# Adding the experts' rows to the residual by an accumulating scatter, with the final norm as a pass of its own

## The chip, the cores and the metric

The kernel runs on one core of a Trainium2 chip. The time is the device time of one execution in microseconds, the median of the runs shown. The engines are TensorE (PE, its weight loads PEld), VectorE (DVE), ScalarE (ACT), GpSimd (POOL) and SyncE (SP); SP, ACT and POOL issue DMAs, which run on the core's 16 DMA engines.

## What is computed

One layer of an encoder on 2048 tokens of 1024 numbers: a norm, a projection, two groups of attention heads, an output projection that is added to the input, and then a mixture of 64 SwiGLU experts. The change touches only what comes after the output projection:

```python
h = h + mixed @ w_out[l]
h = h + hier_moe(rms_norm(h, norm2_gain[l]), ...)      # 8 groups of 8 experts
return rms_norm(h, final_gain)

def hier_moe(x, ...):
    # each token: the best group, in it the best two experts, each with a gate
    expert_id = g_idx[:, None] * EXPERTS_PER_GROUP + top_idx
    ...
    h = silu(xb @ w_gate[e]) * (xb @ w_up[e]); ys = h @ w_down[e]
    y = zeros.at[slot_tok].add(ys * slot_gate[:, None])
```

A token's two experts are always of the same group. The last line makes the output out of the residual plus two gated expert rows.

## The kernel before

The attention stage goes over 16 tiles of 128 tokens and, for each, writes three things to memory: the residual rows (to the output tensor, `out2`, lines 1016 and 1153), the normed rows `d_xn`, and for each of a token's two experts a record in a list `d_list`, which has 100 slots for each expert. A record holds four numbers: the token, the gate, and two flags, "this is the token's last expert" and "its first". `route` (line 1195) works the record out; for the last two tiles the list is made by matmuls (`list_columns`, line 1298), two columns at a time, so that the list `L` is in SBUF when the experts begin.

The expert stage (`experts`, line 1476) goes over 64 experts in an order that visits the eight groups in turn, so that two experts of the same group are eight visits apart. An expert's three weight matrices are 2 MB each and come as six halves of 1 MB (`loads`, into nine `raw` buffers, issued from SP). ScalarE casts a half to `wh`, VectorE subtracts it from the original to give `wl` (`weights`), and TensorE multiplies three times for each product (`products`: `pg`, `pu`, `py`). `inputs` gathers up to 100 normed rows of the expert into `xg` by an indirect DMA from GpSimd and transposes them; `silu` makes `hh` and `hT`.

`sums` (line 1603) closes an expert: it gathers the tokens' rows so far from `out2` into `rg`; VectorE adds the gated product, `r = py * gate + rg`; ScalarE squares `r` and sums, and scales `gf`, the final gain, by the flags; GpSimd makes the norm's factor of the sum with three small instructions; VectorE multiplies, `o = r * ss * o`; and a scatter from GpSimd writes `o` to `out2`. With a first expert the flags make factor and gain one, so that `r` itself is written; with the last one the normed row is written, which is the output. A gather waits for the scatter of the same group's expert before (`data_dep`, eight visits back); the others are declared free of each other.

The order of the instructions on TensorE, VectorE, ScalarE and GpSimd is fixed ahead by `Plan` (line 121): every step is a generator that asks for an engine with a duration and what it needs (`ask`), and `Plan.run` picks the step that can start first. Each engine then works through its list in that order. After the experts, `nblk` says whether any expert had over 100 tokens; a loop for these follows under `tc.If`, and doesn't run with this data.

Of the kernel before, what the change touches and what calls it, by code (L numbers as in the profile page):

```python
# [8 lines left out]
F32 = mybir.dt.float32  # L9
# [19 lines left out]
NG = 8  # L29
# [167 lines left out]
def hybrid_encoder_kernel(ctx, tc, x, norm1_gain, w_in, gla_up_fwd, gla_up_fwd_bias, gla_up_bwd,  # L197
# [20 lines left out]
    L = pers.tile([CAP, NE, 4], I32, name="L")  # L218
# [5 lines left out]
    rec_a = pers.tile([P, NT, 2, 4], I32, name="rec_a")  # L224
# [24 lines left out]
    d_list = scratch("d_list", [LROWS + OROWS, 4], I32)  # L249
# [559 lines left out]
    with ExitStack() as ph:  # L809
# [163 lines left out]
        def project(i, t):  # L973
# [25 lines left out]
            for j in range(2):  # L999
# [16 lines left out]
                nc.sync.dma_start(out2[i * P:(i + 1) * P, j * 512:(j + 1) * 512], hs[j])  # L1016
# [123 lines left out]
        def last_rows(t):  # L1140
# [8 lines left out]
            for j in range(2):  # L1149
# [3 lines left out]
                nc.sync.dma_start(out2[i * P:(i + 1) * P, js], hs[j])  # L1153
# [41 lines left out]
        def route(i, lg, t):  # L1195
# [59 lines left out]
            tr = t  # L1255
            v.tensor_tensor(acc, acc, ob, op=OP.add)
            give(t, f"rank{i - 1}")
            if i in order[-2:]:
# [6 lines left out]
                tr = yield from list_columns(i, 0, o12, at, vals, t, tg)  # L1265
            t = yield ask("dve", 0.7, t, tg)
# [12 lines left out]
            t = yield ask("dve", 0.1, t)  # L1279
# [11 lines left out]
            if i == order[-3]:  # L1291
                t = yield ask("pool", 1.04, t)
                nc.gpsimd.dma_start(L, d_list[0:LROWS].rearrange("(p e) c -> p e c", p=CAP))
                t = yield ask("dve", 0.15, landed(t, 5.0))
                v.tensor_copy(L0, L[:, :, 0])
                give(t, f"list0of{i - 1}", f"list2of{i - 1}")

        def list_columns(i, c0, o12, at, vals, *t):
# [4 lines left out]
            for c in range(2):  # L1303
                src = tok[:, i:i + 1].to_broadcast([P, 2]) if c0 + c == 0 else rows[:, :, c0 + c].bitcast(F32)
                nc.vector.tensor_tensor(vals[:, :, c], o12, src.rearrange("p (k o) -> p k o", o=1).to_broadcast([P, 2, NE]),
                                        op=OP.mult)
            t = yield ask("pe", 0.25, t, take=("pt", f"list{c0}of{i}"))
# [4 lines left out]
            for c in range(2):  # L1312
                src = dst = L[:, :, c0 + c].bitcast(F32)
                if c0 + c == 0:
                    src, dst = L0, L[:, :, 0] if i == last else L0
                nc.vector.tensor_tensor(dst, pt[0:CAP, c], src, op=OP.add)
            give(t, "pt", f"list{c0}of{i - 1}")
# [103 lines left out]
    with ExitStack() as ph:  # L1421
# [5 lines left out]
        xgs, rgs = [], []  # L1427
        for lst, nm in ((xgs, "xg"), (rgs, "rg")):
            for j in range(2):
                t = wp.tile([CAP, D], F32, name=f"{nm}{j}")  # L1430
                nc.gpsimd.memset(t, 0.0)
                lst.append(t)
# [43 lines left out]
        def experts(blocks, ahead=(), then=None):  # L1476


            plan = Plan({"xg": 2, "rg": 2, "xT": 2, "hT": 2, "wh": WN, "wl": WN, "pt": 2, "pg": 1, "pu": 1, "py": PYN,
                         "hh": 2, "r": 2, "o": 2, "visit": NG, "raw": NAHEAD + NB - len(ahead)})  # L1480
            add, give = plan.add, plan.give
            raws, ws, xTs, hTs, ps, nb = {}, {}, {}, {}, {}, len(blocks)
            gets, puts = {}, {}
# [7 lines left out]

            def rows(e, t, out, src):
                return nc.gpsimd.indirect_dma_start(  # L1493
                    out=out, out_offset=None, in_=src, in_offset=bass.IndirectOffsetOnAxis(ap=column(e, 0), axis=0),
                    bounds_check=T - 1, oob_is_err=False)
# [26 lines left out]
            def inputs(e):  # L1522
                xg = xgs[e % 2]
                t = yield ask("pool", 1.95, listed_at, take=("xg",), urge=20.0)
                rows(e, t, xg, d_xn)
# [77 lines left out]
            def sums(e):  # L1603
                rg = rgs[e % 2]
                gate, last, first = (column(e, c) for c in (1, 2, 3))
                t = yield ask("pool", 1.75, listed_at, take=("visit", "rg"), urge=40.0)
                get = rows(e, t, rg, out2)
                for p in range(max(e - NG + 1, 0), e):
                    if p in puts:
                        tc.declare_no_dep(get.ins, puts[p].ins, reason="tokens of other groups")  # L1610
                if e >= NG:
                    tc.add_manual_dep(get.ins, puts[e - NG].ins.name, data_dep, reason="the group's expert before")
                gets[e] = get
                if e + 1 < nb:
                    add(sums(e + 1))
                tr = yield ask("dma", 1.18, (t[0] + 1.5, "pool"), urge=40.0)
                t = yield ask("dve", 1.28, (tr[0] + 1.8, "dma"), take=(f"py{e}", "r"), urge=40.0)
                r = sp.tile([CAP, D], F32, name="r")
                nc.vector.scalar_tensor_tensor(r, ps.pop((e, 2)).rearrange("p a b -> p (a b)"), gate, rg, op0=OP.mult,  # L1619
                                               op1=OP.add)  # L1620
                give(t, "py", "rg")
                o = sp.tile([CAP, D], F32, name="o")
                ss = sp.tile([CAP, 1], F32, name="ss")
                t = yield ask("act", 1.25, t, take=("o",), urge=40.0)
                nc.scalar.activation(o, r, AF.Square, accum_out=ss)
                tg = yield ask("act", 1.24, t, urge=40.0)
# [101 lines left out]
```

## Time and profile before

| | |
|---|---|
| three runs | 3051.7, 3054.0, 3058.02 us; median 3054.0 |
| profiled execution | 3056.35 us, its span 3054.6 us |
| mean granted clock of TensorE | 0.981 |
| busy in the span | PE 93%, DVE 77%, ACT 63%, POOL 27% |
| attention stage | to about 1665 us |
| expert stage | first `xg` transposed at 1702 us, last scatter issued at 3044 us |

In the slices of the page a digit is a busy share in tenths. A row of the timeline has start, duration, engine, line, operation, tiles and shapes; in brackets the idle time of the engine before it and what ended it. A line of the waits has who waited for whom: us in total, times, the longest. A line on a DMA queue has packets, MB and the share of the time of 16 engines that the packets took: q1 is SP's queue, which carries the weights, q0 is GpSimd's, which carries the gathered and scattered rows (it also has packets of 4 bytes, which is why its packets are more than its rows). Stretches for a gather or a scatter were chosen where nothing else was under way on q0.

### The profile page before, as it was taken

The numbers are of one execution on the slowest core, as the hardware profiler recorded it, in microseconds if no ns is written. First come the engines' busy times: TensorE is split into PE (matmuls) and PEld (weight loads), VectorE is DVE, ScalarE is ACT, GpSimd is POOL, SyncE is SP. The second block draws the span as 40 slices with busy tenths as digits, with TensorE's granted clock in tenths as the row PEclk, the third lists the DMA queues.
The fourth block names the chain that finished last, engine by engine and source line by source line (L and its number), as shares of the span: only waits on it lengthen the run. The fifth ranks groups of instructions, "written<-read, shape, count | busy, mean of one in ns | idle before, by whom it ended". The sixth has DMA issues, their size and how long they took to land. (4 is left out here: it accounts for less than half of the span.)

```text
span 3054.6 us, 39259 instructions
## 1 busy us (share of the span) xinstructions
PE 2844.3 (93%) x13784; PEld 2093.0 (69%) x13784; DVE 2365.0 (77%) x3430; ACT 1917.9 (63%) x2872; POOL 810.0 (27%) x575
## 2 busy tenths in 40 slices
PE   7999999999999999999998699899988988988987
PEld 6888788887677777777776466666666666666664
DVE  6554788888667767767776698888888888888886
ACT  4333333333777777777775587777777677777775
POOL 3443111111000000000001354434445444344433
PEclk9999999999999999999998799999999999999998
DMA  7874322223512222112124899999999999999994
GB/s 251 278 269 165 143 96 105 105 77 121 203 56 68 72 68 70 64 61 78 60 72 151 270 342 348 334 344 341 336 337 340 334 334 345 341 335 337 343 325 157
DMA packets 184135, 647.16 MB, mean 212 GB/s; under 512 B 45801, under 2 KB 60489, under 8 KB 130365
## 3 DMA queue, kind: packets, MB, share of 16 engines
q1 hardware_dynamic: 134462, 574.14, 54.3%
q0 software_dynamic: 35008, 51.28, 5.7%
q10 hardware_dynamic: 14464, 19.21, 1.9%
q8 instruction: 109, 1.79, 0.3%
q14 instruction: 92, 0.75, 0.1%
HBM read 563.96 MB, written 108.82 MB: 220 GB/s over the span
## 5 line engine op out<-in xcount | busy, mean ns | idle before, releaser
L1518 DVE TENSOR_TENSOR wl<-raw,wh 128x2048 fp32r<-128x2048 f32 x384 | 872.6, 2286 | 109.8 <-ACT wh L1516 108.1
L1516 ACT CAST wh<-raw 128x2048 fp32r<-128x2048 f32 x384 | 728.7, 1902 | 242.0 <-DMA raw<-in_w_up_dram 83.4
L1353 DVE TENSOR_TENSOR p_l<-p,p_h 128x512 fp32r<-128x512 f32 x512 | 343.7, 688 | 191.7 <-ACT p_h L1350 184.5
L1342 ACT ACTIVATE p<-ps 128x512 f32<-128x512 f32 x512 | 296.1, 599 | 149.1 <-PE ps L1339 130.3
L1563 PE MATMUL pg<-wh,xT 128*100 128x512 f32 x1024 | 357.0, 411 | 0.0
L682 DVE TENSOR_REDUCE nm<-pm 128x1 f32<-128x1024 f32 x256 | 304.8, 1215 | 43.6 <-PE pm L680 43.5
L1563 PE MATMUL pu<-wh,xT 128*100 128x512 f32 x1024 | 332.0, 395 | 0.0
L1569 PE MATMUL py<-wh,hT 128*100 128x512 f32 x1024 | 292.9, 398 | 5.9 <-DVE hT L1599 3.3
L1493 POOL DMA_INDIRECT rg<-out_dram,L x64 | 155.0, 2422 | 511.6 <-DVE r L1619 499.2
L1563 PE MATMUL pg<-wl,xT 128*100 128x512 f32 x512 | 212.0, 414 | 65.9 <-DVE wl L1518 65.6
L1350 ACT CAST p_h<-p 128x512 fp32r<-128x512 f32 x448 | 268.9, 624 | 5.8
L1285 POOL DMA_INDIRECT d_list<-rec_a,di x28 | 28.0, 1000 | 818.2 <-DVE di L1281 813.9
L1563 PE MATMUL pu<-wl,xT 128*100 128x512 f32 x512 | 206.3, 403 | 29.2 <-DVE wl L1518 29.0
L1569 PEld LDWEIGHTS py<-wh,hT 128*100 128x100 f32 x1024 | 167.1, 166 | 74.8 <-DVE hT L1599 7.9
L1563 PEld LDWEIGHTS pg<-wh,xT 128*100 128x100 f32 x1024 | 177.2, 173 | 58.0
L1563 PEld LDWEIGHTS pu<-wh,xT 128*100 128x100 f32 x1024 | 168.9, 165 | 64.0 <-ACT wh L1516 0.2
L1338 PE MATMUL ps<-q,K 128*128 128x512 f32 x512 | 210.6, 411 | 1.5 <-ACT p L1342 1.0
L1364 PE MATMUL pa<-p_h,V 128*66 128x512 f32 x512 | 204.3, 399 | 0.0
L1366 PE MATMUL pa<-p_l,V 128*66 128x512 f32 x512 | 202.7, 396 | 0.9 <-DVE p_l L1353 0.7
L1339 PE MATMUL ps<-q,K 65*128 65x512 f32 x512 | 203.2, 397 | 0.0
L1365 PE MATMUL pa<-p_h,V 128*64 128x512 f32 x512 | 201.6, 394 | 0.0
L1493 POOL DMA_INDIRECT xg<-d_xn,L x64 | 151.6, 2369 | 104.0 <-PE pt L1536 94.9
(426 smaller groups left out, 5730.6 us busy)
## 6 DMA issues: line engine op xcount, KB each, us to landing
raw<-in_w_gate_dram SPq DMA_DIRECT2D x128, 1024.0 KB
raw<-in_w_up_dram SPq DMA_DIRECT2D x128, 1024.0 KB
raw<-in_w_down_dram SPq DMA_DIRECT2D x128, 1024.0 KB
d_uT<-uT SPq DMA_DIRECT2D x16, 1024.0 KB
uT<-d_uT SPq DMA_DIRECT2D x15, 1024.0 KB
x_t<-in_x_dram SPq DMA_DIRECT2D x16, 512.0 KB
wraw<-in_w_in_dram SPq DMA_DIRECT2D x32, 256.0 KB
d_q<-q ACTq DMA_DIRECT2D x16, 512.0 KB
```

The source lines that it names most:

```text
L682: nc.vector.tensor_reduce(nm[:, h, b:b + 1], pm, axis=AX.XY, op=OP.max, negate=True)
L1338: nc.tensor.matmul(ps, lhsT=K1[:, kv, ks], rhs=r1, start=True, stop=False)
L1339: nc.tensor.matmul(ps, lhsT=K2[:, kv, ks], rhs=r2, start=False, stop=True)
L1342: nc.scalar.activation(p, ps, AF.Exp)
L1350: (nc.vector.tensor_copy if hd else nc.scalar.copy)(p_h, p)
L1353: nc.vector.tensor_tensor(p_l, p, p_h.bitcast(F32), op=OP.subtract)
L1364: nc.tensor.matmul(pa, lhsT=hi, rhs=p_h, start=(kt == 0), stop=False)
L1493: return nc.gpsimd.indirect_dma_start(out=out, out_offset=None, in_=src, in_offset=bass.IndirectOffsetOnAxis(ap=column(e, 0), axis=0), bou ...
L1516: nc.scalar.copy(wh, raw)
L1518: nc.vector.tensor_tensor(wl, raw, wh.bitcast(F32), op=OP.subtract)
L1563: nc.tensor.matmul(acc_p, lhsT=xTs[e][:, a, k, :], rhs=w[:, kk, :], start=(k == 0 and a == 0 and w is wh), stop=(k == KD - 1 and a == 1))
L1569: nc.tensor.matmul(acc_p[:, c], lhsT=hTs[e][:, a, k, :], rhs=w[:, kk, c * 512:(c + 1) * 512], start=(k == 0 and a == 0 and w is wh), stop= ...
```

## The change

The residual rows go to a scratch tensor `d_h` instead of the output. `sums` shrinks to two steps: ScalarE reads `py` and scales it by the gate, and GpSimd scatters the result into `d_h` with `compute_op=OP.add`, so that the DMA adds it to the row in memory. The gather of `rg`, the norm and the flags leave it; the record shrinks from four numbers to two, and with it the list and the part of `route` that made the flags. After the experts a new function `finish` loads all of `d_h` in eight transfers of 1 MB into the `raw` buffers, works out the norm of each tile of 128 tokens, and stores 16 tiles to the output.

```diff
-    L = pers.tile([CAP, NE, 4], I32, name="L")
+    L = pers.tile([CAP, NE, 2], I32, name="L")
...
-    rec_a = pers.tile([P, NT, 2, 4], I32, name="rec_a")
+    rec_a = pers.tile([P, NT, 2, 2], I32, name="rec_a")
...
-                nc.sync.dma_start(out2[i * P:(i + 1) * P, js], hs[j])
+                nc.sync.dma_start(d_h[i * P:(i + 1) * P, js], hs[j])
...
-            ov, key = s("ov", 2), s("key", 2)
-            v.tensor_scalar(ov, rk, float(CAP), None, op0=OP.is_ge)
-            v.scalar_tensor_tensor(key, ov, float(NE), eid, op0=OP.mult, op1=OP.add)
-            for c, op in ((2, OP.is_gt), (3, OP.is_lt)):
-                for k in range(2):
-                    v.tensor_tensor(rec[:, k, c:c + 1].bitcast(F32), key[:, k:k + 1], key[:, 1 - k:2 - k], op=op)
-            if i in order[-2:]:
-                t = yield from list_columns(i, 2, o12, at, vals, t)
...
             def sums(e):
-                rg = rgs[e % 2]
-                gate, last, first = (column(e, c) for c in (1, 2, 3))
-                t = yield ask("pool", 1.75, listed_at, take=("visit", "rg"), urge=40.0)
-                get = rows(e, t, rg, out2)
...
-                nc.vector.scalar_tensor_tensor(r, ps.pop((e, 2)).rearrange("p a b -> p (a b)"), gate, rg, op0=OP.mult,
-                                               op1=OP.add)
...
-                nc.scalar.activation(o, r, AF.Square, accum_out=ss)
-                tg = yield ask("act", 1.24, t, urge=40.0)
-                nc.scalar.activation(o, gf[0:CAP], AF.Identity, scale=last, bias=first)
...
-                nc.gpsimd.tensor_scalar(ss, ss, 1.0 / D, EPS, op0=OP.mult, op1=OP.add)
-                nc.gpsimd.tensor_tensor(ss, ss, mhalf[0:CAP, :1], op=OP.pow)
-                nc.gpsimd.tensor_scalar(ss, ss, last, first, op0=OP.mult, op1=OP.add)
-                t = yield ask("dve", 1.28, t, tg, urge=40.0)
-                nc.vector.scalar_tensor_tensor(o, r, ss, o, op0=OP.mult, op1=OP.mult)
...
+                t = yield ask("act", 1.25, take=(f"py{e}", "o"), urge=40.0)
+                o = sp.tile([CAP, D], F32, name="o")
+                nc.scalar.activation(o, ps.pop((e, 2)).rearrange("p a b -> p (a b)"), AF.Identity, scale=column(e, 1))
+                give(t, "py")
...
+                t = yield ask("pool", 2.9, t, take=("visit",), urge=40.0)
                 put = nc.gpsimd.indirect_dma_start(
-                    out=out2, out_offset=bass.IndirectOffsetOnAxis(ap=column(e, 0), axis=0), in_=o, in_offset=None,
-                    bounds_check=T - 1, oob_is_err=False)
+                    out=d_h, out_offset=bass.IndirectOffsetOnAxis(ap=column(e, 0), axis=0), in_=o, in_offset=None,
+                    bounds_check=T - 1, oob_is_err=False, compute_op=OP.add)
...
+        def finish():
+
+            hs = [next_raw(lambda raw, i=i: nc.sync.dma_start(
+                raw.rearrange("p (a d) -> p a d", a=2), d_h[2 * i * P:2 * (i + 1) * P].rearrange("(a p) d -> p a d", p=P)))
+                for i in range(NT // 2)]
+            for i in range(NT):
+                h = hs[i // 2][:, i % 2 * D:(i % 2 + 1) * D]
+                ss = sp.tile([P, 1], F32, name="ss", bufs=4)
+                sq = pp.tile([P, 2, 512], F32, name="py", bufs=PYN)
+                nc.scalar.activation(sq.rearrange("p a b -> p (a b)"), h, AF.Square, accum_out=ss)
+                nc.gpsimd.tensor_scalar(ss, ss, 1.0 / D, EPS, op0=OP.mult, op1=OP.add)
+                nc.gpsimd.tensor_tensor(ss, ss, mhalf[:, :1], op=OP.pow)
+                nc.vector.scalar_tensor_tensor(h, h, ss, gf, op0=OP.mult, op1=OP.mult)
+                nc.sync.dma_start(out2[i * P:(i + 1) * P], h)
+        finish()
```

What stands in a row on three engines changes with it. On GpSimd, from the first gather of the expert stage on, before (`rg` and `xg` have two buffers each, told by their numbers):

```order
L1493 DMA rg_18247<-out_dram,L 100x1024
L1493 DMA rg_18249<-out_dram,L 100x1024
L1493 DMA xg_18243<-d_xn,L 100x1024
L1493 DMA xg_18245<-d_xn,L 100x1024
L1493 DMA xg_18243<-d_xn,L 100x1024
L1493 DMA xg_18245<-d_xn,L 100x1024
L1493 DMA xg_18243<-d_xn,L 100x1024
L1493 DMA rg_18247<-out_dram,L 100x1024
L1629 TENSOR_SCALAR ss<-ss 100x1
L1630 TENSOR_TENSOR ss<-ss,mhalf 100x1
L1631 TENSOR_SCALAR ss<-ss,L 100x1
L1636 DMA out_dram<-o,L 2048x1024
```

and now:

```order
L1507 DMA xg_18102<-d_xn,L 100x1024
L1507 DMA xg_18103<-d_xn,L 100x1024
L1507 DMA xg_18102<-d_xn,L 100x1024
L1507 DMA xg_18103<-d_xn,L 100x1024
L1507 DMA xg_18102<-d_xn,L 100x1024
L1595 DMA d_h<-o,L 2048x1024
L1507 DMA xg_18103<-d_xn,L 100x1024
L1595 DMA d_h<-o,L 2048x1024
```

The two gathers of `rg` ahead of the first `xg` are gone, and from then on one scatter and one gather of `xg` take turns.

On ScalarE, over about one expert in the middle of the stage, before:

```order
L1625 ACTIVATE o,ss<-r 100x1024
L1627 ACTIVATE o<-gf,L 100x1024
L1516 CAST wh<-raw 128x2048 x2
L1541 CAST xT<-pt 128x400
L1516 CAST wh<-raw 128x2048
L1541 CAST xT<-pt 128x400
L1597 CAST hT<-pt 128x400
L1516 CAST wh<-raw 128x2048
L1584 ACTIVATE hh<-pg 100x512
L1516 CAST wh<-raw 128x2048 x2
```

and now:

```order
L1590 ACTIVATE o<-py,L 100x1024
L1498 CAST wh<-raw 128x2048 x3
L1525 CAST xT<-pt 128x400
L1498 CAST wh<-raw 128x2048
L1568 ACTIVATE hh<-pg 100x512
L1525 CAST xT<-pt 128x400
L1581 CAST hT<-pt 128x400
L1498 CAST wh<-raw 128x2048 x2
```

The two passes over `r` and `gf` have become one over `py`; it stands after the expert's last cast, and the casts of the next one follow it.

On SP, at the end of the stage, before (`nblk` and what follows belong to the loop that doesn't run):

```order
L1380 DMA raw<-in_w_down_dram 128x2048 x2
L1380 DMA raw<-in_w_up_dram 128x2048 x2
L1380 DMA raw<-in_w_down_dram 128x2048 x2
L1665 TENSOR_LOAD nblk
L1665 ISA x2
L1666 COMPARE_AND_BRANCH
L1686 COMPARE_AND_BRANCH
```

and now:

```order
L1370 DMA raw<-in_w_down_dram 128x2048 x2
L1370 DMA raw<-in_w_up_dram 128x2048 x2
L1370 DMA raw<-in_w_down_dram 128x2048 x2
L1639 TENSOR_LOAD nblk
L1639 ISA x2
L1625 DMA raw<-d_h 128x2x1024 x8
L1636 DMA out_dram<-raw 128x1024 x16
L1640 COMPARE_AND_BRANCH
```

After the last weights SP now issues eight loads of `d_h`, all of them, and then the 16 stores.

## Rows read from the trace of the kernel before

**Rows 1.** The page's 40 slices: busy tenths, DMA share in tenths, rate.

```profile
PE   7999999999999999999998699899988988988987
DMA  7874322223512222112124899999999999999994
GB/s 251 278 269 165 143 96 105 105 77 121 203 56 68 72 68 70 64 61 78 60 72 151 270 342 348 334 344 341 336 337 340 334 334 345 341 335 337 343 325 157
```

**Rows 2.** Busy time by engine, 200 us each; last columns clock, DMA share, GB/s.

```profile
1800.00:2000.00 200.00, 183.46 (x824) 129.08 (x822) 172.62 (x117) 145.99 (x126) 85.69 (x59) 0.99 1.01 344
...
2200.00:2400.00 200.00, 180.58 (x801) 126.78 (x800) 170.41 (x113) 146.23 (x125) 96.36 (x57) 0.98 0.98 339
...
sum 1000.00, PE 906.20 PEld 634.24 DVE 858.77 ACT 729.57 POOL 447.55; mean PE 181.24 PEld 126.85 DVE 171.75 ACT 145.91 POOL 89.51
```

**Rows 3.** Waits, 1800 to 2900 us: us in total, times, longest.

```profile
ACT wh L1516 <- DMA raw<-in_w_up_dram: 72.5, 73, 3.2
PE pg L1563 <- DVE wl L1518: 61.1, 52, 2.4
...
ACT wh L1516 <- DMA raw<-in_w_down_dram: 52.8, 45, 2.6
ACT wh L1516 <- DMA raw<-in_w_gate_dram: 48.7, 35, 3.8
```

**Rows 4.** Timeline of GpSimd, first and last scatter of the stage.

```profile
1745.82 1.10 POOL L1636 DMA_INDIRECT out_dram<-o,L  x1 [1.64 <-DVE o L1633]
...
3041.57 0.18 POOL L1629 TENSOR_SCALAR ss<-ss 100x1 f32<-100x1 f32 x1 [8.29 <-ACT o L1625]
...
3044.49 1.07 POOL L1636 DMA_INDIRECT out_dram<-o,L  x1 [1.64 <-DVEq L1666]
```

**Rows 5.** DMA packets without rows of tokens, 2522.2 to 2527.2, 2627.1 to 2633.5 us.

```profile
DMA packets 283, 2.06 MB, mean 413 GB/s; under 512 B 32, under 2 KB 32, under 8 KB 32
...
DMA packets 359, 2.65 MB, mean 415 GB/s; under 512 B 35, under 2 KB 35, under 8 KB 35
```

**Rows 6.** DMA queues around a gather, 2210.8 to 2217.3, then 2608.7 to 2615.3 us.

```profile
q1 hardware_dynamic: 211, 1.54, 84.0%
q0 software_dynamic: 136, 0.24, 15.9%
...
q1 hardware_dynamic: 211, 1.53, 81.4%
```

**Rows 7.** DMA queues around a scatter, 2661.6 to 2665.2, then 2363 to 2367 us.

```profile
q1 hardware_dynamic: 166, 1.20, 83.8%
...
q1 hardware_dynamic: 187, 1.35, 84.5%
```

**Rows 8.** Timeline of VectorE, last expert.

```profile
3038.95 1.28 DVE L1619 SCALAR_TENSOR_TENSOR r<-py,L,rg 100x1024 f32<-100x1024 f32 x1 [6.13 <-PE py L1569]
3042.88 1.28 DVE L1633 SCALAR_TENSOR_TENSOR o<-r,ss,o 100x1024 f32<-100x1024 f32 x1 [2.65 <-POOL ss L1631]
```

**Rows 9.** Timeline of ScalarE, last expert.

```profile
3040.32 1.06 ACT L1625 ACTIVATE o<-r 100x1024 f32<-100x1024 f32 x1 [8.88 <-DVE r L1619]
3041.28 0.19 ACT L1625 ACTIVATION_READ_ACCUMULATOR o<-r 100x1 f32 x1
3041.50 1.24 ACT L1627 ACTIVATE o<-gf,L 100x1024 f32<-100x1024 f32 x1
```

**Rows 10.** Timeline of three engines, 1664 to 1703 us.

```profile
1682.24 8.88 DVE L1518 TENSOR_TENSOR wl<-raw,wh 128x2048 fp32r<-128x2048 f32 x4
1683.34 8.72 POOL L1493 DMA_INDIRECT xg<-d_xn,L  x1 [0.30 <-issue]
...
1702.23 0.94 PE L1536 MATMUL pt<-cst_sb,xg 100*128 100x100 f32 x4 [20.39 <-DMA xg<-d_xn,L]
```

**Rows 11.** DMA packets of the last scatter, 3046 to 3048.4 us.

```profile
DMA packets 176, 0.27 MB, mean 111 GB/s; under 512 B 111, under 2 KB 111, under 8 KB 176
```

**Rows 12.** DMA packets of weight loads alone, 1651.5 to 1659.5 us.

```profile
DMA packets 435, 3.19 MB, mean 398 GB/s; under 512 B 47, under 2 KB 47, under 8 KB 47
```

More of the change, by code (lines that the diff above doesn't have):

```diff
@@ L248, in hybrid_encoder_kernel @@
     d_xn = scratch("d_xn", [T, D])
-    d_list = scratch("d_list", [LROWS + OROWS, 4], I32)
+    d_h = scratch("d_h", [T, D])
+    d_list = scratch("d_list", [LROWS + OROWS, 2], I32)
     d_wo = scratch("d_wo", [2, P, KD, D])
@@ L1426, in hybrid_encoder_kernel @@
         nc.scalar.dma_start(gf, bcast_rows(final_gain, D))
[L1427 to L1432, printed above, removed]
+        xgs = [wp.tile([CAP, D], F32, name=f"xg{j}") for j in range(2)]
+        for t in xgs:
+            nc.gpsimd.memset(t, 0.0)
         start = wp.tile([P, NE], F32, name="start")
@@ L1524, in inputs @@
                 t = yield ask("pool", 1.95, listed_at, take=("xg",), urge=20.0)
-                rows(e, t, xg, d_xn)
+                nc.gpsimd.indirect_dma_start(
+                    out=xg, out_offset=None, in_=d_xn, in_offset=bass.IndirectOffsetOnAxis(ap=column(e, 0), axis=0),
+                    bounds_check=T - 1, oob_is_err=False)
                 t = yield ask("dma", 1.18, (t[0] + 1.5, "pool"), urge=20.0)
@@ L1603, in sums @@
             def sums(e):
-                rg = rgs[e % 2]
-                gate, last, first = (column(e, c) for c in (1, 2, 3))
-                t = yield ask("pool", 1.75, listed_at, take=("visit", "rg"), urge=40.0)
-                get = rows(e, t, rg, out2)
[L1608 to L1612, printed above, removed]
@@ L1633, in sums @@
-                nc.vector.scalar_tensor_tensor(o, r, ss, o, op0=OP.mult, op1=OP.mult)
-                give(t, "r")
-                t = yield ask("pool", 2.9, t, urge=40.0)
-                put = nc.gpsimd.indirect_dma_start(
-                    out=out2, out_offset=bass.IndirectOffsetOnAxis(ap=column(e, 0), axis=0), in_=o, in_offset=None,
-                    bounds_check=T - 1, oob_is_err=False)
-                for p in range(max(e - NG + 1, 0), nb):
-                    if p in gets and p != e:
-                        tc.declare_no_dep(put.ins, gets[p].ins, reason="tokens of other groups")
-                    if p in puts:
-                        if e + 1 < nb:
-                            tc.declare_no_dep(put.ins, puts[p].ins, reason="tokens of other groups")
-                        else:
-                            tc.add_manual_dep(put.ins, puts[p].ins.name, data_dep, reason="all rows are done")
+                t = yield ask("pool", 2.9, t, take=("visit",), urge=40.0)
@@ new lines, in sums @@
+                put = nc.gpsimd.indirect_dma_start(
+                    out=d_h, out_offset=bass.IndirectOffsetOnAxis(ap=column(e, 0), axis=0), in_=o, in_offset=None,
+                    bounds_check=T - 1, oob_is_err=False, compute_op=OP.add)
+                for p in range(max(e - NG + 1, 0), e):
+                    if e + 1 < nb:
+                        tc.declare_no_dep(put.ins, puts[p].ins, reason="tokens of other groups")
+                    else:
+                        tc.add_manual_dep(put.ins, puts[p].ins.name, data_dep, reason="all rows are done")
@@ L1647, in sums @@
+                if e >= NG:
+                    tc.add_manual_dep(put.ins, puts[e - NG].ins.name, data_dep, reason="the group's expert before")
                 puts[e] = put
```

45 lines of the change are left out of this document (16 added, 29 removed).

## The prediction

> **What bounds the kernel now.** I read the sliced page first: from about 1740 us to the end the DMA line stands at 9 with 334 to 345 GB/s, beside a PE line of 8 and 9 [rows 1]. This stage, the 64 experts, is where the change lives, so I asked for its busy time in five stretches of 200 us: TensorE 906.2 of 1000 us, VectorE 859, ScalarE 730, GpSimd 448, and a DMA share of 0.98 to 1.01 in each of the five [rows 2]. Three resources are near their limit; which one sets the pace? The waits say it: ScalarE's casts, the first step on every weight, wait 72.5 + 52.8 + 48.7 = 174 us in 1100 us for a weight that has not landed, and TensorE's longest wait (61.1 us, for `wl` at the start of `pg`) is the same lack one step later [rows 3]. So the DMA engines set the pace and TensorE is the next limit, 9% behind. The pace itself: the first scatter is issued at 1745.82 and the 64th at 3044.49, 1298.7 / 63 = 20.6 us for each expert [rows 4]. Busy TensorE is 0.906 x 20.6 = 18.7 us of that.
>
> Then I asked what the DMA engines lose to the rows of tokens. An expert's weights are 6 MB (6.29 million bytes). In two stretches in which no row is under way the weights come at 413 and 415 GB/s [rows 5]: 6.29 MB would take 15.2 us. In two stretches around a gather of `rg`, 1.54 and 1.53 MB of weights took 6.5 and 6.6 us instead of 3.7, so **a gather costs 2.8 to 2.9 us of all 16 engines**, though its 0.24 MB alone are worth 0.6 [rows 6]. In two stretches around a scatter, 1.20 and 1.35 MB took 3.6 and 4.0 us instead of 2.9 and 3.3: **a scatter costs 0.7 us**, its bytes and nothing more [rows 7]. Check: 15.2 + 2 x 2.85 + 0.7 = 21.6 against 20.6 measured, 5% too much; I scale the gather to 2.35 so that the sum fits. Why is a gather so dear? Weights and gathers both write SBUF, a scatter reads it; when the two go the same way both are slow. [...]
>
> **The change part by part.** All against the profiled execution (3056.35 us, span 3054.6; the median of the three runs is 2.4 us under it).
>
> *1. The gather of `rg` goes:* 64 times 2.35 us of the DMA engines. The scatter stays, and becomes an accumulating one. No row shows that. From below it is a scatter, 0.7 us [rows 7] (it can't be less: the same rows go out). From above it is a scatter and a gather, 0.7 + 2.35, if reading the old row hurts the weights as much as `rg` did; more than that only if the engines stand still between read and write. I take twice a scatter, **1.4 us**: the old row has to be read as well as the new one, but nothing is written to SBUF, which is where I put a gather's price, so it is nearer to the scatter [rows 7]. DMA time of an expert: 15.2 + 2.35 (`xg`) + 1.4 = 18.95 us.
>
> *2. Engines.* VectorE loses two passes of 1.28 us for each expert, ScalarE the square (1.06 + 0.19; the pass over `gf`, 1.24, gives way to one that reads `py`), GpSimd three small instructions and the issue of a gather [rows 4, 8, 9]. None of it counts by itself while the weights are late; it lifts VectorE from 86% to some 74%, so that it isn't the next bound. TensorE is: 18.7 us, and I allow 0.2 for waits of its own. DMA 18.95 beside TensorE 18.9, both fed from a pool of nine raw halves: I take **19.3**, 2% above either, for two queues that are nearly even. (20.6 - 19.3) x 64 = **-83 us**. The bounds: a scatter's price gives 18.25 on the DMA side, so TensorE's 18.9 to 19.0 and -102 us; the upper price gives 20.6 and 0.
>
> On GpSimd the new wait is that of the scatter for ScalarE's `o`; queued behind it is the gather of `xg` for a later expert. Before, the scatter stood in the same place and waited for a longer chain (`r`, square, three instructions, `o`), so `xg` moves forward, not back. On ScalarE the casts queue behind `o<-py`, which waits for TensorE; before they queued behind the square, which waited for TensorE and VectorE.
>
> *3. Between the stages.* GpSimd issues two gathers of `rg` ahead of the first `xg`, and that one then takes 8.72 us because VectorE's four subtractions (1682.24, 8.88 us) stand in its way; TensorE waits 20.39 us for it [rows 10]. Without `rg`, and with half of the list's columns, `xg` comes up to 3 us earlier, but the four subtractions start as much earlier. I take **-4 us** (0 to -10, the latter if `xg` slips in ahead of them). In the attention stage six VectorE instructions of under 0.4 us leave each tile; TensorE sets the pace there, so 0 (within 3 us either way, as a few instructions trade places). The stores to `d_h` in place of the output are the same transfers.
>
> *4. The end.* Now: last `r` at 3038.95, scatter issued at 3044.49 [rows 4, 8, 9], its packets between 3046 and 3048.4 [rows 11], and 6.3 us more to the end of the span. After: one ScalarE pass of 1.25 us in place of `r`, square, scale and `o`: the scatter goes out some 3.7 us earlier, its packets take twice as long (+2.2). Then the new pass: eight loads of 1 MB wait until the last scatter has landed, +3 us to the first packet; 8.39 MB in and 8.39 MB out over the same engines, the loads first because they are queued first. At 398 to 415 GB/s [rows 5, 12] 16.8 MB take 40.4 to 42.2; I take 41. Nothing else is left to run beside it. ScalarE's 16 squares (20.0 us) and VectorE's 16 products (20.5) keep step with the loads and hide behind the stores; were loads and stores free, they would still cost 21 + 3. Sum: -3.7 + 2.2 + 3 + 41 = **+42 us** (+36 to +52, the latter at the 340 GB/s of the stage [rows 2]).
>
> **Sum:** 3056.35 - 83 - 4 + 42 = 3011, less 2.4: **3009, say 3010 us**.
>
> **The rivals.** *A, the add is as cheap as a plain scatter.* For it: a scatter takes no more than its bytes' time [rows 7]. Against it: the old row must be read somewhere. TensorE then bounds: 3054 - 102 - 4 + 40 = **2988**.
>
> *B, the read of the old row costs what `rg` cost* (the other side). One mechanism: what makes a gather dear is the reading of scattered rows in memory, not the writing to SBUF. Then the stage keeps its 20.6 us, the pass comes on top: 3054 + 0 - 4 + 42 = **3092**. It decides from the point where the gain in the stage is under 38 us, that is where an accumulating scatter costs over 0.7 + 2.35 - 0.6 = 2.45 us. For it: a gather reads memory and writes SBUF, and its price [rows 6] can't tell the one from the other. Against it: 413 GB/s are read from memory when only weights are read [rows 5], so reading as such is not what is short. [...] No run so far shows an accumulating transfer.
>
> *C, dearer still:* the engines don't overlap the read, the add and the write of one row with the next. At a scatter and two gathers (5.4 us) the stage goes to 23 us: 3054 + 150 + 40 = **3245**.
>
> *D, the stage gains only half*, because TensorE, ScalarE and the DMA engines are all near 19 us and their in-order queues trip over each other: a pace of 20.0 gives -38, and 3054 - 38 - 4 + 42 = **3054**. Against it: VectorE and ScalarE both get room.
>
> That the change doesn't do what it says would be a norm that runs beside the experts after all; it can't, since any group's last expert may touch any tile, and every load waits for the last scatter.
>
> **How the numbers follow.** My forecast (2990 to 3030) 0.50; A 0.12; D 0.08; B 0.18; C 0.12. The likeliest gives 3010. The range runs from A's lower half, 2972, to B's upper side, 3098, and leaves C and a little more out. A measurement of this kernel can't tell 0.2% (6 us) from no change: D gives "same" 0.06, its rest goes half to each side. Faster 0.50 + 0.12 + 0.01 = 0.63; slower 0.18 + 0.12 + 0.01 = 0.31.
>
> **What would show it.** Step 1: the distance of two scatters is 19.3 us (20.6 for B, 19.0 for A, over 22 for C), and the weights keep some 380 GB/s and more while accumulating rows are under way. Step 2: TensorE's busy share in the stage rises from 0.906 to about 0.97, and the waits of casts for weights fall by half. Step 3: TensorE's wait for the first `xg` is 16 us, not 20. Step 4: from the last scatter's landing to the end 50 us instead of 6, with two equal halves of loads and stores at 400 GB/s. I would be wrong if the accumulating scatter holds its engines for over 2.45 us, or if the stores run much slower than the loads.

## The result: 3000 us, and the profile after

The changed kernel takes 3000.0 us (2999.4 to 3000.9) where the one before took 3054.0 in the same comparison: a ratio of 0.982, with an interval of 0.981 to 0.984. The forecast was 3010. The profiled execution has a span of 2997.4 us, 57.2 less than before. I split this at two events that both traces have: TensorE's first transpose of `xg`, and the start of the first pass over the last expert's `py` (`r` on VectorE before, `o` on ScalarE now).

| term | before, us | after, us | difference | predicted |
|---|---|---|---|---|
| to the first `xg` on TensorE | 1702.23 | 1693.69 | -8.5 | -4 |
| from there to the last pass over `py` | 1336.7 | 1249.6 | -87.1 | -83 |
| from there to the end of the span | 15.65 | 54.11 | +38.5 | +42 |
| sum | 3054.6 | 2997.4 | -57.2 | -45 |

The busy time of the stage, in the columns of [rows 2]:

```profile
1800.00:2000.00 200.00, 194.18 (x895) 140.24 (x894) 165.41 (x107) 148.71 (x118) 34.88 (x21) 1.00 1.01 357
...
sum 1000.00, PE 949.70 PEld 682.61 DVE 800.52 ACT 720.49 POOL 179.37; mean PE 189.94 PEld 136.52 DVE 160.10 ACT 144.10 POOL 35.87
```

TensorE went from 906 to 950 of 1000 us, VectorE from 859 to 801, GpSimd from 448 to 179. The DMA share still reads 1, as in [rows 2]. A share of 1 doesn't say by itself that the DMA engines set the pace: in the run `noadd` below it is 1.00 to 1.01 as well, and no cast waits for a weight there.

The waits between 1800 and 2900 us (us in total, times, longest), which answer to [rows 3]:

```profile
ACT wh L1498 <- PE py L1553: 92.7, 55, 4.7
...
PE py L1553 <- ACT hT L1581: 38.4, 54, 2.2
...
ACT wh L1498 <- DMA raw<-in_w_up_dram: 30.9, 34, 2.5
ACT wh L1498 <- DMA raw<-in_w_down_dram: 28.1, 30, 2.0
PE py L1553 <- DVE hT L1583: 13.4, 16, 1.5
```

The casts wait 59 us for weights, not 174. A new wait stands at the top: TensorE wants `hT` at the start of each `py`, 52 us in all, since the transposes of `hh` have moved behind the last of `pg` in TensorE's order. Read by themselves, these rows say that TensorE now bounds the stage. The runs below say that this is not what holds the stage back.

GpSimd's first and last scatter, as in [rows 4], are 1219.7 us apart, 19.36 us for an expert (predicted 19.3):

```profile
1724.96 1.64 POOL L1595 DMA_INDIRECT d_h<-o,L  x1 [5.92 <-ACT o L1590]
...
2944.70 1.58 POOL L1595 DMA_INDIRECT d_h<-o,L  x1 [11.80 <-ACT o L1590]
```

Two stretches with an accumulating scatter and no gather under way on GpSimd's queue, 2800.5 to 2807 and 2841 to 2848 us, chosen where the weights make no pause, read as [rows 7]:

```profile
DMA packets 449, 2.34 MB, mean 359 GB/s; under 512 B 125, under 2 KB 125, under 8 KB 203
...
q1 hardware_dynamic: 276, 2.02, 77.6%
q0 software_dynamic: 173, 0.32, 25.4%
...
DMA packets 516, 2.65 MB, mean 379 GB/s; under 512 B 169, under 2 KB 169, under 8 KB 216
...
q1 hardware_dynamic: 340, 2.46, 86.8%
q0 software_dynamic: 176, 0.19, 14.8%
```

2.02 MB of weights would take 4.87 us at 415 GB/s and took 6.5: 78 rows (the packets between 2 and 8 KB, 203 - 125) cost 1.63 us. 2.46 MB would take 5.93 and took 7.0: 1.07 us for the 47 rows of the smaller scatter. An expert has 64 rows on average, which lies between, near **the 1.4 us that I had taken** as twice a scatter. In six more stretches of this kind, in some of which the weights pause by themselves, the same sum gives 1.05 to 2.55 us, so these two don't fix the price. The runs below bound the add in another way.

The transition, as in [rows 10]: VectorE now has three subtractions in a row there, not four, and `xg` is issued 6.2 us earlier and takes 6.86 us instead of 8.72. It waits for the list `L`, whose last columns are ready 6.0 us earlier (the first two lines are of the kernel before).

```profile
1679.14 0.40 DVE L1316 TENSOR_TENSOR L<-pt,L 100x64 int32<-100x64 f32 x2 [1.33 <-PE pt L1310]
...
1681.88 0.45 DVE L1316 TENSOR_TENSOR L<-pt,L 100x64 f32<-100x64 f32 x2 [1.26 <-PE pt L1310]
...
1675.96 0.36 DVE L1306 TENSOR_TENSOR L<-pt,L 100x64 int32<-100x64 f32 x2 [1.33 <-PE pt L1300]
1676.24 6.68 DVE L1500 TENSOR_TENSOR wl<-raw,wh 128x2048 fp32r<-128x2048 f32 x3
...
1677.12 6.86 POOL L1507 DMA_INDIRECT xg<-d_xn,L  x1 [7.03 <-DVE L L1306]
...
1693.69 0.93 PE L1520 MATMUL pt<-cst_sb,xg 100*128 100x100 f32 x4 [17.77 <-DMA xg<-d_xn,L]
```

And the end, from the last expert on (start, duration; SPq is SyncE issuing):

```profile
2943.29 1.11 ACT L1590 ACTIVATE o<-py,L 100x1024 f32<-100x1024 f32 x1 [5.86 <-PE py L1553]
...
2951.39 7.07 SPq L1625 DMA_DIRECT2D raw<-d_h  x8
2956.36 1.03 ACT L1632 ACTIVATE py<-raw 128x1024 f32<-128x1024 f32 x1 [11.96 <-DMA raw<-d_h]
...
2959.81 6.35 SPq L1636 DMA_DIRECT2D out_dram<-raw  x4
...
2988.52 1.28 DVE L1635 SCALAR_TENSOR_TENSOR raw<-raw,ss,gf 128x1024 f32<-128x1024 f32 x1 [0.72 <-POOL ss L1634]
```

The DMA packets of the two halves of this pass, 2953 to 2973.5 and 2973.5 to 2994 us:

```profile
DMA packets 2146, 8.31 MB, mean 405 GB/s; under 512 B 119, under 2 KB 119, under 8 KB 2144
...
DMA packets 2306, 8.39 MB, mean 409 GB/s; under 512 B 262, under 2 KB 262, under 8 KB 2303
```

Two halves of 20.5 us, the loads at 405 GB/s and the stores at 409, and nothing else under way: the pass is bound by its 16.8 MB, as predicted.

### The profile page after: what moved, and what is told of

Same layout as the page of the kernel before. It is cut to its first block, busy times and chain, and to the rows that moved or that the text cites. A ratio compares the mean times of both kernels' runs of the same rounds, so it can differ in the third digit from the quotient of the medians.

```text
span 2997.4 us, 38671 instructions
## 1 busy us (share of the span) xinstructions
PE 2819.4 (94%) x13776; PEld 2096.9 (70%) x13776; DVE 2222.5 (74%) x3214; ACT 1857.9 (62%) x2776; POOL 468.2 (16%) x349
## 4 chain that ended last, share of the span: by engine, by line
PE 72%; DMA 14%; DVE 5%; ACT 5%; issue 2%; POOL 1%; SPq 0%; ACTq 0%; POOLq 0%; DVEq 0%
PE py L1553 9%; DMA raw<-in_w_up_dram 8%; PE pu L1547 7%; PE pg L1547 7%; PE pm L1007 6%; PE pm L681 4%; PE pa L1356 4%; PE ps L1328 4%; PE pa L1354 4%; PE pa L1355 4%; PE ps L1329 4%; DMA raw<-in_w_down_dram 3%; PE pv L334 3%; PE pqk L334 3%; DVE wl L1500 2%
## 5 line engine op out<-in xcount | busy, mean ns | idle before, releaser
L1553 PE MATMUL py<-wh,hT 128*100 128x512 f32 x1024 | 306.5, 412 | 56.2 <-ACT hT L1581 42.5
L1547 PE MATMUL pg<-wh,xT 128*100 128x512 f32 x1024 | 334.7, 397 | 0.0
L1547 PEld LDWEIGHTS pg<-wh,xT 128*100 128x100 f32 x1024 | 170.5, 167 | 64.1
L1507 POOL DMA_INDIRECT xg<-d_xn,L x64 | 124.9, 1952 | 577.5 <-PE pt L1520 570.2
L1547 PE MATMUL pg<-wl,xT 128*100 128x512 f32 x512 | 202.0, 395 | 0.0
L1595 POOL DMA_INDIRECT d_h<-o,L x64 | 102.1, 1595 | 471.6 <-ACT o L1590 471.6
L681 PE MATMUL pm<-K,q 128*128 128x512 f32 x512 | 169.6, 416 | 1.1 <-DVE nm L683 1.1
```

The lines of the kernel that those rows point to most:

```text
L1547: nc.tensor.matmul(acc_p, lhsT=xTs[e][:, a, k, :], rhs=w[:, kk, :], start=(k == 0 and a == 0 and w is wh), stop=(k == KD - 1 and a == 1))
L1553: nc.tensor.matmul(acc_p[:, c], lhsT=hTs[e][:, a, k, :], rhs=w[:, kk, c * 512:(c + 1) * 512], start=(k == 0 and a == 0 and w is wh), stop= ...
```

## The experiments

All times are to be read against 3000.0 us for the changed kernel; the kernel before was measured beside each group at 3054.8, 3053.1 and 3055.0 us, so the groups can be compared. The changed kernel itself was not run again beside them.

### What gave the stage its gain: the gather, or the engines' work?

The first run puts the gather back into the changed kernel, without anyone who needs it:

```diff
             def sums(e):
+                t = yield ask("pool", 1.75, listed_at, take=("visit", "rg"), urge=40.0)
+                nc.gpsimd.indirect_dma_start(
+                    out=rgs[e % 2], out_offset=None, in_=d_xn, in_offset=bass.IndirectOffsetOnAxis(ap=column(e, 0), axis=0),
+                    bounds_check=T - 1, oob_is_err=False)
+                t = yield ask("dma", 1.18, (t[0] + 1.5, "pool"), urge=40.0)
+                give((t[0] + 1.8, "dma"), "rg")
                 t = yield ask("act", 1.25, take=(f"py{e}", "o"), urge=40.0)
...
-                t = yield ask("pool", 2.9, t, take=("visit",), urge=40.0)
+                t = yield ask("pool", 2.9, t, urge=40.0)
```

> The changed kernel (3000 us) with a gather of the expert's 100 listed rows of d_xn into a buffer that nobody reads, issued ahead of each expert's scatter as before the change; the engines' work stays as changed, the output too. Theory (the stage gained what the gather took from the DMA engines): 15.2 + 2 x 2.35 + 1.4 = 21.3 us for an expert instead of 19.36 measured, +124 us at most, less if the add is cheaper than I took it: 3080 to 3125. Rival (the stage gained because VectorE, ScalarE and GpSimd have less to do): 3000 to 3010.

Measured: **3143.3 us**, 143 more; 2.24 us for each expert. Its busy time and waits (1000 and 1100 us of the stage):

```profile
sum 1000.00, PE 883.46 PEld 626.59 DVE 711.10 ACT 637.46 POOL 229.42; mean PE 176.69 PEld 125.32 DVE 142.22 ACT 127.49 POOL 45.88
```

```profile
PE py L1556 <- ACT hT L1584: 96.7, 49, 4.7
ACT wh L1501 <- DMA raw<-in_w_down_dram: 96.0, 63, 3.8
ACT wh L1501 <- DMA raw<-in_w_up_dram: 78.3, 59, 3.3
```

The waits for weights are back, 174 us in these two rows, and VectorE, with all its relief, is down to 711: it has nothing to work on. The gather takes back more than the 87 us that the stage had gained; the 56 us beyond are 0.9 us for each expert. That is what the add costs over a plain scatter (I had 0.7), if this gather of `d_xn` costs what that of `rg` did, which no run shows by itself. The second run does the opposite, all of the engines' work of before and no gather:

```diff
-                nc.scalar.activation(o, ps.pop((e, 2)).rearrange("p a b -> p (a b)"), AF.Identity, scale=column(e, 1))
+                nc.vector.scalar_tensor_tensor(r, ps.pop((e, 2)).rearrange("p a b -> p (a b)"), column(e, 1), zero,
+                                               op0=OP.mult, op1=OP.add)
...
+                nc.scalar.activation(o, r, AF.Square, accum_out=ss)
...
+                nc.scalar.activation(o, gf[0:CAP], AF.Identity, scale=zero[:, 0:1], bias=first)
...
+                nc.gpsimd.tensor_scalar(ss, ss, 1.0 / D, EPS, op0=OP.mult, op1=OP.add)
+                nc.gpsimd.tensor_tensor(ss, ss, mhalf[0:CAP, :1], op=OP.pow)
+                nc.gpsimd.tensor_scalar(ss, ss, zero[:, 0:1], first, op0=OP.mult, op1=OP.add)
...
+                nc.vector.scalar_tensor_tensor(o, r, ss, o, op0=OP.mult, op1=OP.mult)
```

> The changed kernel with the engines' work of before for each expert (two passes on VectorE, square and scaled gain on ScalarE, three small instructions on GpSimd, with a row of zeros in place of the gathered rows and flags that leave the value as it is), but no gather. Theory (the gather's DMA time is the gain): 3000 to 3020, since TensorE sets the pace and has the engines' work beside it. Rival (relief of the engines): 3070 to 3085, all of the stage's gain given back.

Measured: **2987.3 us** (ratio to before 0.978, 0.976 to 0.981), 13 less than the changed kernel and not more, although VectorE is busy 931 of 1000 us in it. By these two runs the relief of the engines is worth nothing here, and the gather is the whole gain. The busy time, and the first and last scatter:

```profile
sum 1000.00, PE 961.61 PEld 693.73 DVE 930.79 ACT 790.39 POOL 401.90; mean PE 192.32 PEld 138.75 DVE 186.16 ACT 158.08 POOL 80.38
```

```profile
1732.39 1.69 POOL L1613 DMA_INDIRECT d_h<-o,L  x1 [1.64 <-DVE o L1608]
...
2928.93 1.65 POOL L1613 DMA_INDIRECT d_h<-o,L  x1 [1.64 <-DVE o L1608]
```

They are 18.99 us apart for each expert, with the same weights, gathers and accumulating scatters as the changed kernel at 19.36. Why the run is faster stays open. In it the scatter leaves later, and `xg`, which waits behind it on GpSimd, is issued 0.3 to 2.1 us after it and not 9 us or more; and the transposes of `hh` stand earlier in TensorE's order for most experts. The second alone doesn't do it (`hT_mid` below); the first wasn't tried alone.

### What sets the pace now?

The next run takes the add off the scatter (`compute_op=OP.add` is deleted, nothing else; the order of all engines stays). The residual and the token's other expert are then lost from the output.

> The changed kernel with a plain scatter in place of the accumulating one, so that the residual and the token's other expert are lost from the output. Theory (TensorE sets the pace now, 95% busy in the stage): 2985 to 3000, though the DMA engines get the add's 0.65 us for each expert back. Rival (the DMA engines, with a share of 0.99 to 1.01, still set the pace): 0.65 x 64 = 42 us less, 2958.

Measured: **2962.0 us**, 38 less, of which 31 are in the 63 distances from the first scatter to the last. I had expected the other outcome. Its busy time in 1000 us of the stage, TensorE's wait for `hT` in 1100, its first and last scatter, and the stretch 2823.2 to 2827 us around one of its scatters:

```profile
sum 1000.00, PE 967.70 PEld 697.90 DVE 823.75 ACT 739.07 POOL 145.08; mean PE 193.54 PEld 139.58 DVE 164.75 ACT 147.81 POOL 29.02
```

```profile
PE py L1553 <- ACT hT L1581: 32.6, 56, 0.6
```

```profile
1720.35 1.04 POOL L1595 DMA_INDIRECT d_h<-o,L  x1 [5.93 <-ACT o L1590]
...
2908.83 0.98 POOL L1595 DMA_INDIRECT d_h<-o,L  x1 [13.95 <-ACT o L1590]
```

```profile
DMA packets 333, 1.43 MB, mean 376 GB/s; under 512 B 125, under 2 KB 125, under 8 KB 192
...
q1 hardware_dynamic: 157, 1.16, 78.2%
q0 software_dynamic: 176, 0.27, 19.1%
```

The waits list no cast that waits for a weight any more, and TensorE's wait for `hT` is a steady 0.6 us for each expert, the price of the order. This is the kernel at TensorE's own pace, 18.87 us from one scatter to the next (1188.5 us for 63). The add alone makes 19.36 of it, so it costs at least 0.5 us more than a plain scatter, and 0.9 by the run `gather_back`; I had taken 0.7. With no late weights the longest `hT` wait is 0.6 us, where the changed kernel has up to 2.2: on ScalarE a cast of `hT` queues behind the casts of weights, so late weights are likely behind the rest. A plain row holds its packet 19.1% of 16 engines for 3.8 us over 67 rows, 0.17 us; an accumulated one, in the stretch above, 25.4% of 6.5 us over 78, 0.34. Twice, as taken.

Two runs lift TensorE's wait for `hT`. The first puts half of the next `pu` ahead of `py`, in the order of loads, casts and products:

```diff
-    seq = [(0, 0, 0), (0, 0, 1)]
+    seq = [(0, 0, 0), (0, 0, 1), (0, 1, 0)]
     for e in range(n):
-        seq += [(e, 1, 0), (e, 1, 1)] + [(e + 1, 0, 0), (e + 1, 0, 1)] * (e + 1 < n) + [(e, 2, 0), (e, 2, 1)]
+        seq += [(e, 1, 1)] + [(e + 1, 0, 0), (e + 1, 0, 1), (e + 1, 1, 0)] * (e + 1 < n) + [(e, 2, 0), (e, 2, 1)]
```

> The changed kernel with another order of the weight halves: the first half of pu of the next expert comes ahead of py, which gives hT one half more of TensorE's work to be ready in. In the changed kernel TensorE waits for hT at py about 1 us for each expert (the waits show 37.2 + 12.4 us in 1050). Theory (TensorE sets the pace, and these waits are its idle time): 30 to 50 us less, 2950 to 2970. Rival (the DMA engines set the pace): 2995 to 3005.

Measured: **3000.4 us**, no difference. The waits, 1800 to 2900 us:

```profile
ACT wh L1498 <- DMA raw<-in_w_gate_dram: 89.7, 71, 3.5
ACT wh L1498 <- DMA raw<-in_w_up_dram: 82.3, 81, 2.9
ACT wh L1498 <- DMA raw<-in_w_down_dram: 57.8, 58, 2.6
```

TensorE's waits for `hT` are gone and the casts' waits for weights have grown from 59 to 230 us. The wait has only moved to where it comes from. The second run puts the transposes of `hh` half a `pg` earlier, where they stood before the change, for two experts of three:

```diff
+                    if which == 0 and half == 0:
+                        give(t, f"half{e}")
...
-                t = yield ask("pe", 0.42, t, take=("pt", "hT"), urge=20.0)
+                mid = (f"half{e + 1}",) if e + 1 < nb else ()
+                t = yield ask("pe", 0.42, (t[0] - 1.4, t[1]), take=("pt", "hT") + mid, urge=20.0)
```

> The changed kernel with the transposes of hh one half of pg earlier in TensorE's order for two experts of three (where they stood before the change), so that hT is ready when py begins; nothing else is moved on purpose. Theory (the DMA engines need 18.95 us for an expert and TensorE some 18.4 without stalls, and the pace of 19.36 is the two getting in each other's way; the kernel with the old engine work back, which has its transposes there, took 2987): 2978 to 2992. Rival (the DMA engines alone set the pace, as the run with py later seems to say): 2996 to 3003.

Measured: **2998.4 us** (0.980 to 0.983 of before): the rival again. The waits, in the same stretch:

```profile
ACT wh L1498 <- DMA raw<-in_w_up_dram: 110.4, 73, 4.2
ACT wh L1498 <- DMA raw<-in_w_gate_dram: 87.9, 65, 3.0
ACT wh L1498 <- DMA raw<-in_w_down_dram: 42.9, 80, 2.6
PE py L1553 <- DVE hT L1586: 24.3, 33, 1.4
...
PE py L1553 <- ACT hT L1584: 11.1, 15, 1.7
```

TensorE's waits for `hT` fell from 52 to 35 us, the casts' waits for weights rose to 241. So in the changed kernel **the DMA engines still set the pace**, with TensorE 0.5 us behind them: taking TensorE's wait away brings nothing, and taking work off the DMA engines does (`noadd`, and the slots below). The 19.36 us are not the least that its transfers need, though, since `engines_back` carries the same ones in 18.99; how the instructions of the engines lie to each other counts too, and what in it counts wasn't found.

### What the pass at the end costs

The call of `finish()` is left out.

> The changed kernel without the pass at the end: the norm is left out and the output is not written. In the changed kernel 52.7 us lie between the issue of the last scatter and the end, before it was 10.1. Theory (nothing else runs beside the pass): about 43 us less, 2955 to 2962. Rival (part of the 52.7 us is the stage's own tail, which some other wait would show): under 30 us less.

Measured: **2957.9 us**, 42 less. Its last scatter is issued at 2944.44, within 0.3 us of the changed kernel's, so the stage is the same, and the difference is the pass.

### Where a gather's price lies

The prediction put the price of a gather on the writing of SBUF. If that is so, the partitions that it writes may count as well, which no run so far shows. Four runs carry a dummy transfer of 64 rows (0.26 MB) for each expert in the place of `gather_back`'s, which nobody reads; only its list and its destination differ. The first two, with a list of their own that doesn't change:

```diff
+        lst = wp.tile([96, 1], I32, name="lst")
+        nc.gpsimd.memset(lst, BIG)
+        nc.gpsimd.iota(lst[0:64], pattern=[[0, 1]], base=0, channel_multiplier=32)
```

and in the second, in place of the last line,

```diff
+        nc.gpsimd.iota(lst[0:32], pattern=[[0, 1]], base=0, channel_multiplier=32)
+        nc.gpsimd.iota(lst[64:96], pattern=[[0, 1]], base=1024, channel_multiplier=32)
```

> The changed kernel with a dummy gather for each expert whose list has 64 fixed rows of d_xn, 32 apart, for partitions 0 to 63, and nothing for partitions 64 to 95; nobody reads it. It is the counterpart of the next run. Theory: as the gather of the expert's own list, 3080 to 3125. If the lists' own spread of tokens or the length of 100 made the price, less.

Measured: **3141.1 us**, 2.20 us for each gather, as the expert's own list (2.24).

> The same 64 rows gathered into partitions 0 to 31 and 64 to 95 instead of 0 to 63. If the price of a gather comes from the half of the partitions that it writes (the reading of my prediction), the price falls by half: some 40 to 60 us less than the run before it. If it comes from reading rows in memory or from the list, the two runs agree within 8 us. [...]

Measured: **3118.8 us**, 1.86 us for each gather. The placement alone changes the time, by 22 us, but by a sixth and not by half; the half was my guess, with no run behind it.

The other two have no list; the first line is that of `load_plain`, the second that of `load_128`, whose buffer has 128 partitions of 512 numbers:

```diff
+                nc.gpsimd.dma_start(rgs[e % 2][0:64], d_xn[0:64])
...
+                nc.gpsimd.dma_start(rgs[e % 2], d_xn[0:64].rearrange("r (a c) -> (r a) c", a=2))
```

> The changed kernel with an ordinary load of 64 rows of d_xn that stand in a row into partitions 0 to 63, on the same queue from GpSimd, for each expert, in place of the dummy gather. If the price of a gather is its bytes and its writing of SBUF, as the gather, +80 to +125 us; if it comes from the list (packets made one by one from it), the bytes alone are left, 0.26 MB or 0.6 us for each expert: 3000 to 3040.

Measured: **3165.5 us**, 2.59 us for each load. It isn't the list, and it isn't scattered rows in memory: 64 rows that stand in a row are dearer still.

> The changed kernel with the ordinary load of 0.26 MB on GpSimd's queue for each expert as in the run load_plain, but as 128 pieces of 2 KB, one in each partition, in place of 64 rows of 4 KB in partitions 0 to 63. Nobody reads it. If the price (2.6 us for each load there) comes from which partitions are written: 0.6 to 1 us for each, 3030 to 3065. If it comes from packets of a second queue among the weights, whatever they write: 3130 to 3170, with the packets of half the size rather dearer than cheaper.

Measured: **3047.6 us**, 0.74 us for each load. The same 0.26 MB out of the same rows, over 128 partitions instead of 64. The DMA packets of the two runs, 1800 to 2800 us:

```profile
DMA packets 58280, 318.87 MB, mean 319 GB/s; under 512 B 15073, under 2 KB 15073, under 8 KB 23714
...
DMA packets 63904, 349.37 MB, mean 349 GB/s; under 512 B 16576, under 2 KB 16576, under 8 KB 26021
```

For each MB moved in all there are (23714 - 15073) / 318.87 = 27.1 packets between 2 and 8 KB in the first and (26021 - 16576) / 349.37 = 27.0 in the second: the dummy load comes in as many packets in both. So the price hangs on how the same bytes lie on the partitions, 4 KB on each of 64 or 2 KB on each of 128. The number of partitions and the bytes on each changed together, and no run takes them apart. A change of the partitions alone, with 4 KB on each of 64 (`gather_low` to `gather_spread`), took 0.34 us off 2.20; the step from `load_plain` to `load_128` took 1.85 off 2.59. What the rest of that step comes from no run here shows.

The placement can be used. A list's slots are put on other partitions, so that the 64 rows of a usual expert come into partitions 0 to 31 and 64 to 95 (`SLOTS` holds first partition, first slot and their number):

```diff
+SLOTS = (0, 0, 32), (32, 64, 32), (64, 32, 32), (96, 96, 4)
...
+    for p, r, n in SLOTS:
+        nc.gpsimd.iota(iota_s[:, p:p + n], pattern=[[1, n]], base=r, channel_multiplier=0,
+                       allow_small_or_imprecise_dtypes=True)
...
-                    v.tensor_scalar(at[:, k], iota_c, rk[:, k:k + 1], None, op0=OP.is_equal)
+                    v.tensor_scalar(at[:, k], iota_s, rk[:, k:k + 1], None, op0=OP.is_equal)
...
-                nc.gpsimd.dma_start(L, d_list[0:LROWS].rearrange("(p e) c -> p e c", p=CAP))
+                for p, r, n in SLOTS:
+                    nc.gpsimd.dma_start(L[p:p + n], d_list[r * NE:(r + n) * NE].rearrange("(p e) c -> p e c", p=n))
```

> The changed kernel with the list's slots put on other partitions: slots 32 to 63 stand on partitions 64 to 95, and 64 to 95 on 32 to 63, so that the 64 rows of a usual expert come into partitions 0 to 31 and 64 to 95. With the dummy gather this placement took 22 us off (3141 to 3119), 0.35 us for each gather. Theory: the same 0.35 us of the DMA engines for xg; where weights are late it shows in full, where TensorE waits for hT it doesn't: 2978 to 2993. Rival (the placement did something only for a gather that ran beside the scatter): 2998 to 3003.

Measured: **2982.4 us** (ratio to before 0.977, 0.975 to 0.979), 18 less than the changed kernel. Its scatters are 19.13 us apart, 0.23 less for each expert, which makes 14 of the 18; the expected 0.35 was too much. TensorE is busy 956 of 1000 us, and the casts' waits for weights are 35 us in 1000:

```profile
ACT wh L1504 <- DMA raw<-in_w_down_dram: 18.2, 23, 1.8
ACT wh L1504 <- DMA raw<-in_w_up_dram: 17.0, 19, 1.6
```

```profile
1722.21 1.63 POOL L1601 DMA_INDIRECT d_h<-o,L  x1 [5.94 <-ACT o L1596]
...
2927.68 1.58 POOL L1601 DMA_INDIRECT d_h<-o,L  x1 [11.80 <-ACT o L1596]
```

> Both of the two edits before: transposes of hh earlier, list slots spread. Theory (two limits that lie side by side, each edit lifts one): more than either, 2960 to 2978. Rival (only one of the limits counts): the better one of the two runs before.

Measured: **2981.0 us** (0.975 to 0.979), with the edits of the two runs together: no more than the slots alone, as the rival has it. With the slots spread the kernel beats both kernels of the comparison, by 18 to 19 us and by some 73.

## Why the prediction was right

**Step 1, the gather and the add.** The gather's 2.35 us, scaled down so that the sum fits, was 2.24 when it was put back. The add at twice a scatter, 1.4 us, was 1.07 and 1.63 in two stretches with fewer and more rows than average (1.05 to 2.55 over all eight that were read), and by the runs 1.2 to 1.6. The price held better than my reason for it. I had written that weights and gathers are slow because both write SBUF; `load_128` writes as much as a gather and costs 0.74 us, about its bytes (0.26 MB at 415 GB/s are 0.63), while the same bytes into 64 partitions cost 2.59. So it isn't writing as such that is dear, but something in how 64 partitions are written. A scatter, which only reads them, cost 0.7 [rows 7]. That an add is cheap because it writes no SBUF fits, and no run tests it alone. And which 64 partitions are written is only a part of the price: 0.34 us of 2.20 (`gather_spread`).

**Step 2, the pace.** TensorE's 18.9 us showed as 18.87 when the DMA engines left it alone (`noadd`), and the pace is 19.36 for the 19.3 that I took. The 0.35 us between 18.95 and 19.3 came from no row, and that they fit is in part luck: with another order of the engines' work the same transfers run at 18.99 (`engines_back`). Of the signs that I had named two missed here. TensorE's share is 0.95, not 0.97: I had divided the busy time of before, 18.7 us, by the new pace, but of 19.36 us it is now busy 18.4. VectorE's 74% has the same kind of slip, reckoned over the old pace of 20.6 us: over 19.3 it makes 78%, and 80% were measured. And weights beside accumulating rows move at 311 and 351 GB/s, not 380: 1.4 us out of 6.5 leave 326 of 415, which I could have worked out from my own price. The waits for weights fell to a third rather than half.

**Step 3, the transition.** -8.5 us instead of -4. `xg` was issued 6.2 us earlier where I had up to 3, and the subtractions that it ends behind are three and not four: before, they ended at 1691.12 and `xg`'s issue at 1692.06 [rows 10], now at 1682.92 and 1683.98. I had assumed that the four stay four. Half of the list's columns made 2.8 of the 6.2: before, the flags' columns were ready at 1682.33, behind the others at 1679.54. The rest came earlier, where I had put 0: these others are ready 3.2 us sooner, at 1676.32. TensorE waited 17.8 us for `xg`, not the 16 that I had named, since it too was done sooner. The sum is inside the bound that I gave (0 to -10).

**Step 4, the end.** +38.5 instead of +42. From the pass over `py` to the scatter's issue 1.4 us instead of 5.5 (-4.1 for -3.7); its packets end some 6 us after the issue instead of 4 (+2.2 as taken); 41 us of transfers were 41. The 3 us from there to the first load came from no row and were some 2. What I left out: of the 6.3 us that stood behind the last scatter before, only some 3 stand behind the last store; so from the scatter's landing to the end it is some 47 us, not the 50 that I had named.

**The rivals.** *A* (an add as cheap as a scatter) falls by `noadd`: the add costs 38 us. *B* (the read of the old row costs what `rg` cost) would have left 20.6 us for an expert; what is dear isn't the read, since `load_128` reads the same rows as `load_plain` and costs 0.74 us to its 2.59. An accumulated row does hold its packet twice as long as a plain one, 0.34 us against 0.17. It doesn't follow that the add is as dear as a gather: beside the accumulating rows the weights went on at 311 and 351 GB/s, around a gather at 237 and 232 [rows 6]. *C* (23 us, 3244 by its own sum and not 3245) and *D* (20.0 us, no gain) are excluded by the pace. D came nearest: the transposes of `hh` did move behind `pg` and made a new wait, but a wait that cost nothing while the weights were late.

## What to carry to other kernels

Here, where weights come at 413 to 415 GB/s when no rows of tokens are under way [rows 5], a gather of some 64 rows into 64 partitions costs nearly four times its bytes' time (2.24 us for 0.6), and an accumulating scatter about twice a plain one (1.2 to 1.6 us for 0.7); trading the first for the second paid, even with a pass of 16.8 MB at the end (42 us). How a small transfer's bytes lie on the partitions is worth a run of its own (2.59 us or 0.74 here). And a wait at the top of the list names the bound only if lifting it moves the time: here TensorE waited most for `hT`, but a kernel without that wait was no faster (3000.4 us, `py_later`), and the same lateness came out as waits for weights.

## What the runs showed that I had not expected

An ordinary load of 64 rows into partitions 0 to 63 costs 2.59 us of the weights' time, and 0.74 us when the same bytes go to 128 partitions. The accumulating scatter takes GpSimd 1.6 us to issue in the changed kernel, the plain one of `noadd`, in the same order of instructions, 1.0. And in the last pass a GpSimd instruction on 128 numbers takes 1.28 us beside VectorE's product and 0.19 before the products begin:

```profile
2957.61 0.19 POOL L1633 TENSOR_SCALAR ss<-ss 128x1 f32<-128x1 f32 x1 [11.32 <-ACT py L1632]
...
2962.51 1.28 DVE L1635 SCALAR_TENSOR_TENSOR raw<-raw,ss,gf 128x1024 f32<-128x1024 f32 x1 [0.72 <-POOL ss L1634]
2962.56 1.28 POOL L1633 TENSOR_SCALAR ss<-ss 128x1 f32<-128x1 f32 x1
```

The 16 products are paced at 2.0 us by it, from 2958.50 to 2988.52, and don't keep step with the loads as I had thought; the stores, at 409 GB/s, hide it.
